# Down projection of a hybrid encoder block: more pairs of k-tiles by seven block products, and one low part per pair made by an adding transfer

## The chip, the cores and the metric

The kernel runs on one core of one Trainium2 chip. The metric is device time in microseconds of one execution. The profile of an execution gives its span (from the first to the last instruction), which is a little shorter than the time of the same execution.

## The reference

One layer of an encoder block on 256 tokens of width 2048, all in float32: a mixer (input projection, a state-space scan in two directions, a pooling mixer, output projection), a gated feed-forward with a short convolution, and a gated per-layer embedding. Each part ends in an RMS norm and is added to the residual. The change touches the down projection of the feed-forward, a product of (256 x 5632) and (5632 x 2048):

```python
def conv_glu(hn, w_up, conv_w, conv_b, w_down):
    up = hn @ w_up
    gate, val = jnp.split(up, 2, axis=-1)
    gate = dwconv_centred(gate, conv_w, conv_b)
    return (jax.nn.gelu(gate, approximate=True) * val) @ w_down
```

## The kernel before

**Products in two parts.** TensorE multiplies float32r, a shorter format. Every operand x is split into a high part (x rounded) and a low part (x minus the high part), and a product is the sum of three: high by high, high by low, low by high. `split` (L138) does this for weights: ScalarE writes the high part (L147), VectorE subtracts (L148). High and low parts go to two rings of five buffers each (tags whi and wlo), 1024 columns wide.

**Down projection.** `sublayer` (L701) is called for it at L827. It makes the 2048 output columns in two halves of 1024 (`dn0` and `dn1` in the profile's names). In each half `token_major` (L240) goes through the 44 tiles of 128 rows of the weight in 22 pairs. One pair is one load of 1 MB by SyncE (`raw`, L151, three buffers; the transfer is issued at L118). 128 tokens are one block of an activation tile, so a pair of k-tiles is a 2 x 2 by 2 x 2 block product: two token halves, two k-tiles, two column halves of 512.

**Eight or seven products.** An ordinary pair takes eight block products. With three matmuls each that is 24 matmuls of 128 x 128 by 128 x 512, in the order of the k-tiles (L256 to L262). The pairs named in `fast` go to `seven_products` (L201), a Strassen-like scheme with 21 matmuls: the first split (a, L206) and the second (b, L207) take parts of the weight as they are, then VectorE forms three differences in place in the raw buffer (L209 to L211), and two more splits (c and d) take the results. The partial sums go to the accumulators `acc` and to four more (`alt`), which `combine` (L222) adds up. The combination stands behind the pair after the last fast one; that pair, and the last of the half, run output tile by output tile (first case of the order at L256), so both k-tiles are wanted early.

**Activations.** `get_hid` (L779) makes high and low parts of the hidden activations for one pair: ScalarE copies (L783), VectorE subtracts (L784), in a tile `hs` with two buffers. Seven-product pairs also need sums of token blocks: `hid_sums` (L800) makes them with four small VectorE steps (L812 to L815, tile `hd`) and splits them (L817, L818). Those of the first four fast pairs are kept for the second half of the columns (tile `hsum`), others are made anew (tile `he`).

**Order.** Each engine runs its instructions in an order fixed when the program is built, by a scheduler with estimated costs; an instruction that waits holds up all behind it on its engine. GpSimd issues no transfer; during the down projection it does next to nothing.

Of the kernel before, what the change touches and what calls it, by code (L numbers as in the profile page):

```python
# [12 lines left out]
F32R = mybir.dt.float32r  # L13
AF = mybir.ActivationFunctionType
ALU = mybir.AluOpType

P = 128
# [6 lines left out]
NF = DFF // P  # L24
# [27 lines left out]
def build(nc, a, out):  # L52
# [5 lines left out]
    with tile.TileContext(nc) as tc, \  # L58
# [8 lines left out]
        def ins(r):  # L67
            return getattr(r, "ins", r)

        def page(name, dtype=F32):  # L70
            return gp.tile([P, 2048], dtype, tag="pg", bufs=13, name=name)
# [4 lines left out]
        def tiny(name, n=2):  # L76
            return sp.tile([P, n], F32, tag="tiny", bufs=40, name=name)

        def main(name):
            return [pm.tile([P, 512], F32, tag="main", name=f"{name}_{i}") for i in range(2)]  # L80

        def misc(name):
            return pc.tile([P, 512], F32, tag="misc", name=name)

        def mm(o, lhsT, rhs, start, stop):
            nc.tensor.matmul(o, lhsT, rhs, start=start, stop=stop, skip_group_check=True)  # L86
# [17 lines left out]
        acc, acc2 = [main(f"dtu{t}") for t in range(2)], main("dtu2")  # L104
# [10 lines left out]
        def load(dst, src, ahead=False):  # L115

            with tc.issue_after(last["dma"]) if last and not ahead else nullcontext():
                return ins(nc.sync.dma_start(dst, src))  # L118
# [17 lines left out]
        spare = {}  # L136

        def split(name, src, nel, cuts=()):  # L138

            if name in spare:  # L140
                hi, lo = spare.pop(name)
            else:
                hi = wp.tile([P, 1056], F32R, tag="whi", bufs=5, name=f"{name}h")
                lo = wp.tile([P, 1056], F32R, tag="wlo", bufs=5, name=f"{name}l")
            for c0, c1 in zip((0, *cuts), (*cuts, nel)):
                s = slice(c0, c1)
                last["act"] = ins(nc.scalar.copy(hi[:, s], src[:, s]))  # L147
                last["dve"] = ins(nc.vector.tensor_sub(lo[:, s], src[:, s], hi[:, s].bitcast(F32)))  # L148
            return hi, lo

        def raw(name, src, a_, b_):  # L151
            r = wp.tile([P, 2048], F32, tag="raw", bufs=3, name=name)
            last["dma"] = load(r[:, :a_ * b_].rearrange("p (a b) -> p a b", a=a_), src, True)
            return r
# [34 lines left out]
        def aside():  # L189

            for job in (work.pop(0) if work else ()):
                job()

        def columns(acc):

            c = 0
            for o in acc:
                yield o, c
                c += o.shape[-1]

        def seven_products(name, r, a_, acc, alt, start, stop):  # L201

            v = r.rearrange("p (b c) -> p b c", b=4)
            b11 = split(f"{name}a", r[:, :512], 512)  # L206
            b2 = split(f"{name}b", r[:, 1024:], 1024)  # L207

            nc.vector.tensor_sub(v[:, 0:2], v[:, 1::2], v[:, 0:2])  # L209
            nc.vector.tensor_sub(v[:, 3], v[:, 3], v[:, 0])  # L210
            nc.vector.tensor_sub(v[:, 2], v[:, 2], v[:, 3])  # L211
            t13 = split(f"{name}c", r[:, :1024], 1024)
            t42 = split(f"{name}d", r[:, 1024:], 1024)
            for x, (wh, wl), c, o, own in (
                    ("a11", b11, 0, alt[0], True), ("a12", b2, 0, acc[0][0], False), ("s4", b2, 512, acc[0][1], False),
                    ("s1", t13, 0, alt[1], True), ("s3", t13, 512, alt[2], True), ("a22", t42, 0, acc[1][0], False),
                    ("s2", t42, 512, alt[3], True)):
                xh, xl = a_[x]
                for q, (xx, ww) in enumerate(((xh, wh), (xh, wl), (xl, wh))):
                    mm(o, xx, ww[:, c:c + 512], own and start and q == 0, own and stop and q == 2)  # L220
# [16 lines left out]
            add(s165, alt[2], s165)  # L237
            add(acc[1][1], acc[1][1], s165)

        def token_major(name, w, c0, ks, get, acc, tail=1, fast=(), alt=None, sums=None):  # L240


            group, nu = [], len(ks) // 2
            for u in range(nu):
                k0 = ks[2 * u]
                r = raw(f"{name}r{k0}", w[k0 * P:(k0 + 2) * P, c0:c0 + 1024]
                        .rearrange("(k p) c -> p k c", p=P), 2, 1024)
                if u in fast:
                    seven_products(f"{name}{k0}", r, sums(k0), acc, alt, u == fast[0], u == fast[-1])
                    continue  # L250
                for j in range(2):
                    group.append((k0 + j, *split(f"{name}{k0}_{j}", r[:, j * 1024:(j + 1) * 1024], 1024)))
                if nu - tail <= u < nu - 1:
                    continue

                order = [(t, o, g, q) for t in range(2) for o in columns(acc[t]) for g in group for q in range(3)] \  # L256
                    if u == nu - 1 or u - 1 in fast[-1:] else \
                    [(t, o, g, q) for g in group for t in range(2) for q in range(3) for o in columns(acc[t])]
                for t, (o, c), (k, wh, wl), q in order:
                    xh, xl = (v[:, t * P:(t + 1) * P] for v in get(k))  # L260
                    xx, ww = ((xh, wh), (xh, wl), (xl, wh))[q]
                    mm(o, xx, ww[:, c:c + o.shape[-1]], k == ks[0] and q == 0, k == ks[-1] and q == 2)  # L262
                if u - 1 in fast[-1:]:
                    combine(name, acc, alt)
                group = []
                aside()
# [121 lines left out]
        for u in range(0, NK, 2):  # L388
            r = [wp.tile([P, 2048], F32, tag="raw", bufs=3, name=f"dtur{u}") if u else r0, page(f"dtur{u + 1}")]
            for j in range(2):  # L390
                k = u + j
# [17 lines left out]
            for j in range(2):  # L409
                k = u + j  # L410
                with tc.issue_after(front[0]), tc.issue_after(front[1]):
                    wh, wl = split(f"dtu{k}", r[j][:, :1056], 1056, ((352, 704), (704,))[k] if k < 2 else ())
                if k == 8:
                    half = last["act"], last["dve"]
# [250 lines left out]
        for t in range(2):  # L665
# [13 lines left out]
            r = rms(f"yn{t}", [ss], rz[t][:, 1:2], n=2)  # L679
# [18 lines left out]
            load(g, src.partition_broadcast(P))  # L698
            return g

        def sublayer(name, w, ks, get, gain, h, vnext, panel=Panel, fast=((), ()), sums=None):  # L701

            mg = [page(f"{name}m{t}") for t in range(2)]
            sq = [[], []]
            for half in range(2):

                alt = main(f"{name}s{half}") if fast[half] and half == 0 else []
                acc = [main(f"{name}a{half}{t}") for t in range(2)]
                if fast[half]:
                    alt += (main(f"{name}s{half}") if half else []) + [misc(f"{name}s{half}_{i}") for i in (2, 3)]  # L710
                token_major(f"{name}{half}", w, half * 1024, ks, get, acc, 1, fast[half], alt, sums)
                for t in range(2):
                    for n in range(2):
                        q = tiny(f"{name}q{t}{half}{n}", 1)
                        junk = sp.tile([P, 512], F32, tag="junk", bufs=1, name=f"{name}j{t}{half}{n}")
                        c = slice(half * 1024 + n * 512, half * 1024 + (n + 1) * 512)
                        b = acc[t][n]
                        nc.scalar.activation(junk, b, AF.Square, accum_out=q)
                        nc.vector.tensor_mul(mg[t][:, c], b, gain[:, c])
                        sq[t].append(q)  # L720
            r = [rms(f"{name}{t}", sq[t], 1.0 / D) for t in range(2)]
            pan = panel(f"{name}x")
            for c in range(4):
                s = slice(c * 512, (c + 1) * 512)
                for t in range(2):
                    nc.vector.scalar_tensor_tensor(h[t][:, s], mg[t][:, s], r[t], h[t][:, s],  # L726
                                                   op0=ALU.mult, op1=ALU.add)
                panel_part(f"{name}x", pan, h, vnext, 4 * c, 4 * c + 4)
            return pan
# [15 lines left out]
        h = [page(f"h{t}") for t in range(2)]  # L745
# [10 lines left out]
        for s in range(DFF // 512):  # L756
            sc = mid(f"gr{s}")
            for i in range(2):
                ga = main(f"ga{s}{i}")
                feature_pairs(f"ug{s}{i}", w_up, s * 512 + i * 256, hf, ga)  # L760
                o = sc[:, i * 512:(i + 1) * 512]
# [7 lines left out]
            for i in range(2):  # L769
                va = main(f"va{s}{i}")  # L770
                feature_pairs(f"uv{s}{i}", w_up, DFF + s * 512 + i * 256, hf, va)
                c0 = (s % 2) * 1024 + i * 512
# [27 lines left out]
        def hid_sums(k):  # L800
# [20 lines left out]
            else:  # L821
# [3 lines left out]
            return d  # L825

        hp = sublayer("dn", w_down, list(range(NF)), hid_get, gload("gffn", a["ffn_norm_post"][0]), h, V_PN,  # L827
                      fast=((2, 5, 8, 11, 14, 17), (2, 5, 8, 11, 14, 17, 19)), sums=hid_sums)


        pl.append(ple(1))
# [32 lines left out]
        for half in range(2):  # L864
            acc = [main(f"gt{half}{t}") for t in range(2)]
# [9 lines left out]
            for t in range(2):  # L875
                for n, (o, c0) in enumerate(columns(acc[t])):
                    c1 = c0 + o.shape[-1]
                    c = slice(half * 1024 + c0, half * 1024 + c1)
# [63 lines left out]
```

## Time and profile before

| | |
|---|---|
| median of 3 runs | 1146.65 us (1146.38 to 1147.1) |
| the profiled execution's own time | 1147.28 us |
| its span | 1145.5 us |
| mean granted TensorE clock | 0.994 |
| the down projection's matmuls on the chain of waits | from 801.24 to 1034.06 us |
| HBM read | 215.95 MB |

Times are microseconds from the start of the span. PE is TensorE, PEld its weight loads, DVE is VectorE, ACT ScalarE, POOL GpSimd, SP SyncE; `L86` is a line of the kernel, and as one helper records all matmuls, they are told apart by their tiles (`dna` the accumulators `acc`, `dns` those of `alt`). "x48" is a count. In a row of the chain of waits the first two numbers are start and duration; in a row of a time line a bracket names idle time before the instruction and what ended it. In a row of the groups of one tile, three durations in ns are the least, the median and the greatest.

### The profile page before, as it was taken

How to read it: one execution, taken by the hardware profiler on the slowest of the kernel's cores; microseconds unless marked ns; L12 is line 12 of the kernel's file. 1: busy time of each engine (PE TensorE's matmuls, PEld its weight loads, DVE VectorE, ACT ScalarE, POOL GpSimd, SP SyncE). 2: the span in 40 equal slices, each digit the busy share in tenths (PEclk: the TensorE clock that was granted, in tenths of full speed). 3: DMA queues.
4: the chain of work that ended last, by engine and by line, in shares of the span. 5: the costliest groups of instructions: out<-in, count | busy, mean ns of one | idle time of the engine just before them, and what ended most of it. 6: DMA issues, size and time to landing. Idle time of an engine off the chain costs nothing.

```text
span 1145.5 us, 15408 instructions
## 1 busy us (share of the span) xinstructions
PE 1126.3 (98%) x6057; PEld 971.6 (85%) x6057; DVE 824.8 (72%) x1060; ACT 598.3 (52%) x812; POOL 122.5 (11%) x123
## 2 busy tenths in 40 slices
PE   9998999999999999999999999999999999999996
PEld 9997987888888888888888888888888888887885
DVE  6578896654777665666766766668888888898573
ACT  7533543553675454544544545545555556657462
POOL 0274504200110000000000000000000000002001
PEclk9998999999999999999999999999999999999998
DMA  9952347546365555555555565556466646564752
GB/s 358 337 184 74 111 150 267 201 156 216 121 213 186 192 192 195 190 185 184 184 187 193 181 207 189 184 184 221 159 209 221 204 163 221 187 206 159 226 179 74
DMA packets 129592, 219.03 MB, mean 191 GB/s; under 512 B 3696, under 2 KB 96752, under 8 KB 128624
## 3 DMA queue, kind: packets, MB, share of 16 engines
q1 hardware_dynamic: 129232, 217.70, 57.4%
q8 instruction: 47, 0.77, 0.3%
q10 hardware_dynamic: 288, 0.36, 0.1%
q14 instruction: 25, 0.20, 0.1%
HBM read 215.95 MB, written 2.10 MB: 190 GB/s over the span
## 4 chain that ended last, share of the span: by engine, by line
PE 92%; DVE 5%; POOL 1%; ACT 1%; issue 1%; POOLq 0%; DVEq 0%; ACTq 0%
PE va L86 21%; PE ga L86 21%; PE dna L86 17%; PE woa L86 8%; PE gt L86 7%; PE dtu L86 4%; PE z L86 4%; PE xbc L86 3%; PE dns L86 3%; DVE cv L373 2%; DVE w L586 1%; DVE xb_0l L148 1%; PE ple L86 1%; PE yd L86 0%; DVE h L726 0%
## 5 line engine op out<-in xcount | busy, mean ns | idle before, releaser
L86 PE MATMUL ga<-wox,ug_0h 128*128 128x512 f32 x352 | 125.5, 395 | 0.0
L86 PE MATMUL ga<-wox,ug_1h 128*128 128x512 f32 x352 | 125.1, 394 | 0.0
L86 PE MATMUL va<-wox,uv_0h 128*128 128x512 f32 x352 | 124.8, 393 | 0.0
L86 PE MATMUL va<-wox,uv_1h 128*128 128x512 f32 x352 | 124.8, 393 | 0.0
L86 PE MATMUL ga<-wox,ug_0l 128*128 128x256 f32 x352 | 99.1, 282 | 0.0
L86 PE MATMUL ga<-wox,ug_1l 128*128 128x256 f32 x352 | 99.1, 282 | 0.0
L86 PE MATMUL va<-wox,uv_0l 128*128 128x256 f32 x352 | 99.1, 281 | 0.0
L86 PE MATMUL va<-wox,uv_1l 128*128 128x256 f32 x352 | 99.1, 281 | 0.0
L86 PEld LDWEIGHTS va<-wox,uv_0h 128*128 128x128 f32 x352 | 66.1, 188 | 15.0
L86 PEld LDWEIGHTS va<-wox,uv_1h 128*128 128x128 f32 x352 | 66.1, 188 | 15.0
L86 PEld LDWEIGHTS ga<-wox,ug_1h 128*128 128x128 f32 x352 | 66.1, 188 | 14.9
L86 PEld LDWEIGHTS ga<-wox,ug_0h 128*128 128x128 f32 x352 | 66.1, 188 | 14.8
L86 PE MATMUL dna<-dn_0h,hs 128*128 128x512 f32 x248 | 75.8, 393 | 0.0
L86 PE MATMUL dna<-dn_1h,hs 128*128 128x512 f32 x248 | 75.6, 393 | 0.0
L767 POOL TENSOR_TENSOR fc<-fc,rfb 128x1024 f32<-128x1024 f32 x11 | 26.4, 2404 | 440.2 <-ACT fc L766 440.2
L86 PEld LDWEIGHTS ga<-wox,ug_0l 128*128 128x128 f32 x352 | 66.2, 188 | 0.1
L86 PEld LDWEIGHTS ga<-wox,ug_1l 128*128 128x128 f32 x352 | 66.2, 188 | 0.0
L86 PEld LDWEIGHTS va<-wox,uv_0l 128*128 128x128 f32 x352 | 66.2, 188 | 0.0
L86 PEld LDWEIGHTS va<-wox,uv_1l 128*128 128x128 f32 x352 | 66.2, 188 | 0.0
L86 PEld LDWEIGHTS dna<-dn_1h,hs 128*128 128x128 f32 x248 | 46.5, 188 | 10.8
L86 PEld LDWEIGHTS dna<-dn_0h,hs 128*128 128x128 f32 x248 | 46.5, 188 | 10.7
L86 PE MATMUL dna<-dn_0l,hs 128*128 128x512 f32 x124 | 40.2, 393 | 0.0
(1075 smaller groups left out, 2860.3 us busy)
## 6 DMA issues: line engine op xcount, KB each, us to landing
dn0r<-w_ffn_down SPq DMA_DIRECT2D x22, 1024.0 KB, 5.5
dn1r<-w_ffn_down SPq DMA_DIRECT2D x22, 1024.0 KB, 5.5
zr<-w_in SPq DMA_DIRECT2D x8, 1024.0 KB, 5.2
wo0r<-w_out SPq DMA_DIRECT2D x8, 1024.0 KB, 5.6
wo1r<-w_out SPq DMA_DIRECT2D x8, 1024.0 KB, 5.5
gt0r<-w_ple_gate SPq DMA_DIRECT2D x8, 1024.0 KB, 6.0
gt1r<-w_ple_gate SPq DMA_DIRECT2D x8, 1024.0 KB, 5.6
dtur<-w_in SPq DMA_DIRECT2D x14, 528.0 KB, 8.6
```

The source lines that it names most:

```text
L86: nc.tensor.matmul(o, lhsT, rhs, start=start, stop=stop, skip_group_check=True)
L148: last["dve"] = ins(nc.vector.tensor_sub(lo[:, s], src[:, s], hi[:, s].bitcast(F32)))
L373: nc.vector.scalar_tensor_tensor(o[:, lo:hi], i[:, lo + d:hi + d], vec(wcol + j * wstep + f), o[:, lo:hi], op0=ALU.mult, op1=ALU.add)
L586: nc.vector.scalar_tensor_tensor(w[:, h * P:(h + 1) * P], cbm[:, 0, g, t, :], dt[:, t, 8 * g + h:8 * g + h + 1], w[:, h * P:(h + 1) * P], ...
L767: nc.gpsimd.tensor_tensor(cv.rearrange("p (f t) -> p f t", f=4), cv.rearrange("p (f t) -> p f t", f=4), rfb.unsqueeze(1).to_broadcast([P, ...
```

## The change

Three things change, all in the down projection.

- The lists `fast` name 9 and 10 pairs for 6 and 7: every second pair from 2 to 18 in both halves, and 19 in the second.
- The new list `far` names pairs 2 to 21 of the first half and all of the second. In these, one split of 1024 columns per pair, the second k-tile's (in a seven-product pair the split b), is made by the new function `split_far`: ScalarE writes the negated rounded weight into the low buffer, GpSimd issues a transfer of 512 KB that reads the same weights from HBM again and adds them to it, and ScalarE writes the high part. VectorE has no step in this split.
- `token_major` and `sublayer` hand the list on.

```diff
+        def split_far(name, src, far, nel):
...
+                hi = wp.tile([P, 1056], F32R, tag="whi", bufs=5, name=f"{name}h")
+                lo = wp.tile([P, 1056], F32R, tag="wlo", bufs=5, name=f"{name}l")
+            nc.scalar.activation(lo[:, :nel], src[:, :nel], AF.Copy, scale=-1.0)
+            o = lo[:, :nel]
+            if len(far.shape) == 3:
+                o = o.rearrange("p (k c) -> p k c", k=far.shape[1])
+            nc.gpsimd.dma_start(o, far, accum_op=ALU.add)
+            nc.scalar.copy(hi[:, :nel], src[:, :nel])
+            return hi, lo
...
-            b2 = split(f"{name}b", r[:, 1024:], 1024)
+            b2 = split(f"{name}b", r[:, 1024:], 1024) if far is None else split_far(f"{name}b", r[:, 1024:], far, 1024)
...
                 if u in fast:
-                    seven_products(f"{name}{k0}", r, sums(k0), acc, alt, u == fast[0], u == fast[-1])
+                    seven_products(f"{name}{k0}", r, sums(k0), acc, alt, u == fast[0], u == fast[-1],
+                                   w[(k0 + 1) * P:(k0 + 2) * P, c0:c0 + 1024] if u in far else None)
                     continue
                 for j in range(2):
-                    group.append((k0 + j, *split(f"{name}{k0}_{j}", r[:, j * 1024:(j + 1) * 1024], 1024)))
+                    k, s = k0 + j, r[:, j * 1024:(j + 1) * 1024]
+                    group.append((k, *(split_far(f"{name}{k0}_{j}", s, w[k * P:(k + 1) * P, c0:c0 + 1024], 1024)
+                                       if j and u in far else split(f"{name}{k0}_{j}", s, 1024))))
...
-                      fast=((2, 5, 8, 11, 14, 17), (2, 5, 8, 11, 14, 17, 19)), sums=hid_sums)
+                      fast=((2, 4, 6, 8, 10, 12, 14, 16, 18), (2, 4, 6, 8, 10, 12, 14, 16, 18, 19)), sums=hid_sums,
+                      far=(range(2, NF // 2), range(NF // 2)))
```

More of the change, by code (lines that the diff above doesn't have):

```diff
@@ L149, in split @@
             return hi, lo
+        def split_far(name, src, far, nel):
+            if name in spare:
+                hi, lo = spare.pop(name)
+            else:
+                hi = wp.tile([P, 1056], F32R, tag="whi", bufs=5, name=f"{name}h")
[7 more added lines that the diff above has]
+            return hi, lo
         def raw(name, src, a_, b_):
@@ L199, in columns, with seven_products @@
                 c += o.shape[-1]
-        def seven_products(name, r, a_, acc, alt, start, stop):
+        def seven_products(name, r, a_, acc, alt, start, stop, far):
             v = r.rearrange("p (b c) -> p b c", b=4)
             b11 = split(f"{name}a", r[:, :512], 512)
-            b2 = split(f"{name}b", r[:, 1024:], 1024)
+            b2 = split(f"{name}b", r[:, 1024:], 1024) if far is None else split_far(f"{name}b", r[:, 1024:], far, 1024)
             nc.vector.tensor_sub(v[:, 0:2], v[:, 1::2], v[:, 0:2])
@@ L238, in combine, with token_major @@
             add(acc[1][1], acc[1][1], s165)
-        def token_major(name, w, c0, ks, get, acc, tail=1, fast=(), alt=None, sums=None):
+        def token_major(name, w, c0, ks, get, acc, tail=1, fast=(), alt=None, sums=None,
+                        far=()):
             group, nu = [], len(ks) // 2
@@ L699, in gload, with sublayer @@
             return g
-        def sublayer(name, w, ks, get, gain, h, vnext, panel=Panel, fast=((), ()), sums=None):
+        def sublayer(name, w, ks, get, gain, h, vnext, panel=Panel, fast=((), ()), sums=None, far=((), ())):
             mg = [page(f"{name}m{t}") for t in range(2)]
@@ L710, in sublayer @@
                     alt += (main(f"{name}s{half}") if half else []) + [misc(f"{name}s{half}_{i}") for i in (2, 3)]
-                token_major(f"{name}{half}", w, half * 1024, ks, get, acc, 1, fast[half], alt, sums)
+                token_major(f"{name}{half}", w, half * 1024, ks, get, acc, 1, fast[half], alt, sums, far[half])
                 for t in range(2):
```

## The prediction

> **What bounds the kernel now.** I read the page first, then the chain of waits in order of time, then the table of stretches, and only then the two engines that prepare the weights.
>
> ```profile
> span 1145.5 us, 15408 instructions
> PE 1126.3 (98%) x6057; PEld 971.6 (85%) x6057; DVE 824.8 (72%) x1060; ACT 598.3 (52%) x812; POOL 122.5 (11%) x123
> GB/s 358 337 184 74 111 150 267 201 156 216 121 213 186 192 192 195 190 185 184 184 187 193 181 207 189 184 184 221 159 209 221 204 163 221 187 206 159 226 179 74
> PE va L86 21%; PE ga L86 21%; PE dna L86 17%; PE woa L86 8%; PE gt L86 7%; PE dtu L86 4%; PE z L86 4%; PE xbc L86 3%; PE dns L86 3%; DVE cv L373 2%; DVE w L586 1%; DVE xb_0l L148 1%; PE ple L86 1%; PE yd L86 0%; DVE h L726 0%
> ```
>
> TensorE is busy for 98% of the span, and the chain that ended last runs through matmuls. The down projection is "PE dna" and "PE dns" in it, a fifth of the span. Here are one ordinary stretch (two eight-product pairs) and one seven-product pair, then the table of stretches for the same 16 us and for the whole stage:
>
> ```profile
> 849.06 11.11 PE dna L86 x48
> 860.17 0.70 PE dns L86 x3
> 860.86 1.38 PE dna L86 x6
> 862.24 1.39 PE dns L86 x6
> 863.62 0.69 PE dna L86 x3
> 864.31 0.69 PE dns L86 x3
> ```
>
> ```profile
> 849.06:865.00 15.94, 15.94 (x70) 12.95 (x70) 13.21 (x15) 9.28 (x12) 0.00 (x0) 1.00 0.60 197
> 790.00:1035.00 245.00, 245.00 (x1078) 199.81 (x1077) 214.45 (x263) 145.37 (x186) 1.29 (x4) 1.00 0.59 193
> ```
>
> In the second fence the columns are PE, PEld, DVE, ACT and POOL busy, then the granted clock, DMA share and GB/s. TensorE has no gap at a clock of 1.00, so one matmul is worth 11.11 / 48 = 0.231 us. An eight-product pair (24 matmuls) takes 5.55 us, a seven-product pair (21) 4.85 us. VectorE is at 13.21 of 15.94: it is the engine with least room. The stage ends with TensorE, so only matmuls or new gaps between them change the time.
>
> **The change, part by part.** *Matmuls.* Six more pairs (13 to 19) lose three matmuls each: 18 x 0.231 = **4.2 us less**. That is all there is to win; everything else can only hold or spoil it. The two combinations stay.
>
> *VectorE.* Its rows inside one seven-product pair, where starts lie closer than durations:
>
> ```profile
> 850.55 0.68 DVE L784 TENSOR_TENSOR hs<-hid,hs 128x512 fp32r<-128x512 f32 x1
> 851.16 0.68 DVE L148 TENSOR_TENSOR dn022al<-dn0r,dn022ah 128x512 fp32r<-128x512 f32 x1
> 851.88 1.23 DVE L209 TENSOR_TENSOR dn0r<-dn0r 128x1024 f32<-128x1024 f32 x1
> 853.02 1.22 DVE L148 TENSOR_TENSOR dn022bl<-dn0r,dn022bh 128x1024 fp32r<-128x1024 f32 x1
> 854.27 0.69 DVE L210 TENSOR_TENSOR dn0r<-dn0r 128x512 f32<-128x512 f32 x1
> 855.00 0.69 DVE L211 TENSOR_TENSOR dn0r<-dn0r 128x512 f32<-128x512 f32 x1
> ```
>
> A 1024-wide step takes 1.14 us of the engine (851.88 to 853.02), a 512-wide one 0.61 (850.55 to 851.16). The new repeat is one eight-product and one seven-product pair, 45 matmuls, 10.40 us. VectorE does in it 1.14 + 0.61 for the first and 0.61 x 4 + 0.12 (a small gap) + 1.14 x 3 for the second: 7.7 us; with the two low parts that the transfer now makes it would be 10.0. Pairs whose token sums are not kept add some 1.5 us: those steps are 284 and 686 ns long:
>
> ```profile
> L812 DVE TENSOR_TENSOR hd<-hid x9: 281/284/291, 771.0 to 919.1; 128x128 f32<-128x128 f32 x9
> L818 DVE TENSOR_TENSOR he<-hd,he x5: 682/686/693, 808.8 to 1001.4; 128x512 fp32r<-128x512 f32 x5
> L817 ACT CAST he<-hd x5: 605/620/622, 807.0 to 999.6; 128x512 fp32r<-128x512 f32 x5
> ```
>
> That gives 9.2 of 10.40, and would be 11.5 without the transfer. So VectorE stays hidden, and the transfer is what makes room for the six pairs.
>
> *ScalarE.* It gains a negated copy per pair, 42 in all. Its rows:
>
> ```profile
> 854.65 0.62 ACT L783 CAST hs<-hid 128x512 fp32r<-128x512 f32 x1 [1.72 <-PE dna L86]
> 855.17 1.05 ACT L147 CAST dn022ch<-dn0r 128x1024 fp32r<-128x1024 f32 x1
> 860.25 1.05 ACT L147 CAST dn_0h<-dn0r 128x1024 fp32r<-128x1024 f32 x1 [1.72 <-PE dna L86]
> 861.20 1.04 ACT L147 CAST dn_1h<-dn0r 128x1024 fp32r<-128x1024 f32 x1
> 862.15 0.61 ACT L783 CAST hs<-hid 128x512 fp32r<-128x512 f32 x1
> ```
>
> By starts, 0.96 us for 1024 and 0.52 for 512. Per 10.40 us: seven wide and three narrow copies, 8.3 us (8.8 with sums). It fits if it rarely waits.
>
> *The new wait.* The low part used to be ready one VectorE step after the high part. Now it is ready after a copy and a transfer of time T (from the copy's end to the landing, GpSimd's issue included). Buffers are few, so this closes a loop. In the changed program's order, ScalarE in a seven-product pair makes the activations' copy (hs, two buffers) ahead of the negated copy. The row at 854.65 shows what hs waits for: TensorE's end of the pair two before, 849.06 + 5.55 = 854.61. Behind it on ScalarE stand the negated copy and c and d. In the new order the pair two before is the previous seven-product pair. From its end to the end of the next one: hs 0.52, negated copy 1.05, T, then the 17 matmuls from the first that reads the low part (the fifth) to the last, 3.93, and some 0.15 for three hand-overs (0.04 at 854.65). So **the repeat is never shorter than T + 5.65**, and TensorE sees nothing while T is below 10.40 - 5.65 = **4.75 us**. The eight-product pairs form a second loop through the five high buffers: 0.95 + 0.96 + 1.05 + T + 10 matmuls 2.31 + 0.2 = T + 5.47, nearly the same. They run in parallel, so the larger counts, not the sum.
>
> *T.* No transfer here adds, and none is issued by GpSimd. The nearest rows:
>
> ```profile
> dn0r<-w_ffn_down SPq DMA_DIRECT2D x22, 1024.0 KB, 5.5
> dn1r<-w_ffn_down SPq DMA_DIRECT2D x22, 1024.0 KB, 5.5
> out<-vg SPq DMA_DIRECT2D x8, 256.0 KB, 2.7
> gffn<-ffn_norm_post SPq DMA_DIRECT2D x1, 1024.0 KB, 8.9
> ```
>
> A plain 512 KB lies between 256 KB and 1 MB: 2.7 + 2.8 / 3 = 3.6 us, the lower end. An adding one also reads its 512 KB destination, so its engines read 1 MB: 5.5 us, the nearest row. GpSimd's issue, and the weight load that starts in the same moment (SyncE's load waits for the last read of the same raw buffer, which is now the negated copy), come on top. The upper end is 8.9, the slowest 1 MB of this stretch. I take the middle, **6.25 us**, a little over the nearest row.
>
> The Trainium skill, DMA: Bandwidth & Descriptors, section "Anatomy of one DMA — SWDGE (gpsimd) path", gives a GpSimd DMA 2.0 us plus bytes / 436e3; an estimate from it for 512 KB is 3.2 us, and by it no repeat would stall. Collectives: The Full Stack, section "The bandwidth ceiling", says that an adding transfer reads two sources on the same ring and so runs at half rate; the estimate becomes 4.4 us, still just under the loop's limit. Against that, the same fit gives 4.4 us for 1 MB where this trace's row has 5.5; no run so far shows the adding itself.
>
> *The sum.* At T = 6.25 each of the 18 seven-product pairs in the alternation (nine per half) pays 6.25 - 4.75 = 1.5 us: 27 us. The pair after the alternation (19 in the first half, 20 in the second) is worked through tile by tile, so its second low part is wanted at the fifth matmul instead of the fifteenth, 2.3 us earlier, with the copies of the second loop ahead of it: 4.85 + 0.92 - 3.1 leaves T = 2.7 without a wait. Two such pairs pay 3.5 each: 7 us. The first pairs of the halves and the last pair I set at nothing, because buffers are free or two plain pairs lie between; uncovered, each costs another 1.5. Together 27 + 7 - 4.2 = **+30 us**. The profiled execution took 1147.28 us (span 1145.5); the median shown is 1146.65. So 1177.3 against the first, **1177** against the median.
>
> **The rivals.** *1. The transfer is hidden (the other side).* Where T stays under 4.75 no alternating pair waits; the two pairs at the ends pay T - 2.7 each. At the lower end, 3.6, that is 1.8 - 4.2 = -2.4 us, 1144.2; at 4.75 it is 4.1 - 4.2, no change, 1146.5; if the ends are covered too, the whole 4.2, 1142.5. It decides at T = 4.75. For it: DMA engines are busy only 0.59 of the stage. Against it: the plain 1 MB row is over the limit already. The page's fit of 3.2 to 4.4 us leads here. 22%: 14% faster, 8% no change.
>
> *2. Bytes instead of latency.* A repeat then moves two loads of 1 MB and two adding transfers that read 1 MB each, 4.2 MB; at 358 GB/s, the most that any slice of the page shows, 11.7 us. That is 1.3 us over 10.40 in some 20 repeats: +26 - 4.2, 1168; no gap would have one latency to blame, and the loads would land late as well. 12%.
>
> *3. ScalarE becomes the bound.* It has 8.8 us of work, and the two waits of 1.72 us shown above come on top if they stay: 12.2 a repeat, 1.8 x 20 - 4.2, 1179. Against it: these waits are slack in front of free buffers today. 5%.
>
> *4. A slow T that is still paid in part by slack*, between 4.75 and 5.2: 1147 to 1157. 6%, a third of it no change.
>
> **How the numbers follow.** The forecast has 55%: T from 5.2 to 8.9, 1157 to 1230 (18 x 4.15 + 2 x 6.2 - 4.2 = +83). The range runs from the whole gain, 1143, to T of about 8.6, 1225; a slower transfer and the last half microsecond of the gain are left out, some 10%. Measurement here tells 0.2%, 2.3 us, from no change. Faster 14%; no change 8 + 2 = 10%; slower 76%.
>
> **What would show it.** In the changed profile: the GpSimd transfers' time to landing (42 of 512 KB) over 4.75 us confirms the price, under it rival 1. TensorE waits before a matmul that reads a low part, released by a DMA, about 1.5 us each, in the seven-product pairs; ends of 48 or 24 matmuls moving apart from 5.55 us. VectorE must fall from 13.21 per 15.94 us to about 0.75 to 0.9 of the time or less, or its part is wrong. Rival 2 shows as a DMA share near 0.9 and loads above 8 us; rival 3 as ScalarE without idle time. I am wrong if T is short, if the loop through hs is not closed (the negated copy ahead of hs), or if GpSimd's transfers hold each other up in their queue, which would lie above my range.

## The result, and the profile after

| | before | after |
|---|---|---|
| median, us | 1146.66 (1146.38 to 1147.1, 4 runs) | 1277.21 (1276.0 to 1278.98, 4 runs) |
| ratio to before, 95% interval | | 1.1139 (1.112 to 1.1159) |
| span of the profiled execution, us | 1145.5 | 1274.2 |
| mean granted TensorE clock | 0.994 | 0.955 |
| down projection on the chain, us | 801.24 to 1034.06 (232.8) | 800.72 to 1165.16 (364.4) |

The changed kernel is 11.4% slower. The sign was forecast; the size was not: 1277 lies far above the forecast 1177 and above the range, which ended at 1225. All of the loss is in the down projection, which takes 131.6 us longer.

From the page of the changed kernel: busy time, granted clock, the queue of GpSimd's transfers, and the DMA issues with their median time to landing; then TensorE's waits in the down projection (us in total, times, longest):

```profile
PE 1162.7 (91%) x6039; PEld 992.6 (78%) x6039; DVE 813.1 (64%) x1078; ACT 648.2 (51%) x872; POOL 159.1 (12%) x165
PEclk9998999999999999999999999999887878889998
q0 software_dynamic: 6048, 22.02, 8.9%
dn0r<-w_ffn_down SPq DMA_DIRECT2D x22, 1024.0 KB, 7.1
dn_1l<-w_ffn_down POOLq DMA_DIRECT2D x23, 512.0 KB, 9.4
```

```profile
PE dna L86 <- DMA dn_1l<-w_ffn_down: 90.2, 19, 6.3
PE dna L86 <- DMA dn138bl<-w_ffn_down: 2.0, 1, 2.0
```

TensorE runs 18 matmuls fewer (6039), yet shows 36 us more of busy time, because its clock falls: the digits 8 and 7 near the end of the clock's row lie in the down projection. It waits 90.2 us for the low part `dn_1l` (the one that the eight-product pairs now get by transfer) and only once in a seven-product pair (`dn138bl`), where the prediction had expected the waits. The adding transfer takes 9.4 us to land. The loads of 1 MB, at 5.5 us before, take 7.1. On the chain of waits, which consisted of matmuls, one pattern repeats:

```profile
815.13 4.31 DMA dn_1l<-w_ffn_down
...
950.32 8.77 DMA dn_1l<-w_ffn_down
```

The chain goes from transfer to transfer. Between them it reads "issue" for some 12 us each (rows left out here), so it gives the length of a repeat but not what closes it; the time line below shows that. In the first half eight repeats lie between 815.13 and 950.32, 16.90 us each, where 45 matmuls are 10.40 us of work. One repeat in the time line, all engines (start, duration, engine, line, operation; the bracket names idle time before it and what ended it):

```profile
881.87 0.37 SPq L118 DMA_DIRECT2D dn0r<-w_ffn_down  x1
882.14 0.87 POOL L162 DMA_DIRECT2D dn_1l<-w_ffn_down  x1 [12.49 <-ACT dn_1l L158]
885.60 0.87 POOL L162 DMA_DIRECT2D dn024bl<-w_ffn_down  x1 [2.59 <-ACT dn024bl L158]
891.54 0.72 PE L86 MATMUL dna<-dn_1l,hs 128*128 128x512 f32 x2 [4.64 <-DMA dn_1l<-w_ffn_down]
892.10 1.86 PE L86 MATMUL dna<-dn_1h,hs 128*128 128x512 f32 x4
899.01 0.87 POOL L162 DMA_DIRECT2D dn_1l<-w_ffn_down  x1 [12.54 <-ACT dn_1l L158]
```

A load of 1 MB goes out at 881.87, the adding transfer 0.27 us behind it, a second adding transfer 3.5 us later. The first lands at 891.54, 9.40 us after its issue, and TensorE has stood still for 4.64 us. Then four matmuls take 1.86 us, twice their usual 0.93. The stretches of this repeat and the one before show both (PE, PEld, DVE, ACT and POOL busy, then clock, DMA share, GB/s):

```profile
865.32:882.14 16.82, 12.23 (x47) 9.48 (x46) 8.01 (x9) 8.39 (x11) 1.74 (x2) 0.90 0.73 188
878.70:882.10 3.40, 3.40 (x16) 2.76 (x15) 1.23 (x1) 3.21 (x4) 0.00 (x0) 1.00 0.03 11
886.00:891.00 5.00, 0.91 (x4) 0.38 (x3) 4.31 (x8) 1.80 (x3) 0.47 (x1) 1.00 1.02 220
892.00:893.00 1.00, 1.00 (x5) 0.77 (x4) 0.00 (x0) 0.00 (x0) 0.00 (x0) 0.57 1.05 242
893.00:894.00 1.00, 1.00 (x4) 0.81 (x3) 0.00 (x0) 0.00 (x0) 0.00 (x0) 0.50 1.02 385
894.00:895.00 1.00, 1.00 (x3) 0.76 (x3) 0.00 (x0) 0.00 (x0) 0.00 (x0) 0.50 1.01 418
895.00:896.00 1.00, 1.00 (x5) 0.77 (x4) 0.00 (x0) 0.25 (x1) 0.00 (x0) 0.72 0.49 201
```

The DMA engines are full (1.02) while TensorE waits and nearly empty (0.03) just before the next transfer is issued: transfers bunch. After the gap the granted clock is 0.57, 0.50, 0.50 and 0.72 for four microseconds, which loses 0.43 + 0.50 + 0.50 + 0.28 = 1.7 us. So a repeat costs 16.87 - 10.40 = 6.5 us: 4.64 of waiting, 1.7 of slow matmuls, and a little for the hand-over.

The whole stage, in the same columns (the prediction shows this row for the kernel before, 790.00 to 1035.00):

```profile
790.00:1168.00 378.00, 285.83 (x1075) 224.42 (x1074) 206.44 (x286) 197.65 (x251) 41.53 (x52) 0.86 0.72 186
```

TensorE stands still for 378.00 - 285.83 = 92.2 us, in 20 gaps of 2.0 to 6.4 us. In the 364.4 us of the down projection it is therefore busy for 272.2 us, with matmuls that take 232.8 - 4.2 = 228.6 us at full clock. So 43.6 us go to the slower clock.

### The profile page after: what moved, and what is told of

It is laid out like the page before. It is cut to its first block, busy times and chain, and to the rows that moved or that the text cites. A ratio compares the mean times of both kernels' runs of the same rounds, so it can differ in the third digit from the quotient of the medians.

```text
span 1274.2 us, 15613 instructions
## 1 busy us (share of the span) xinstructions
PE 1162.7 (91%) x6039; PEld 992.6 (78%) x6039; DVE 813.1 (64%) x1078; ACT 648.2 (51%) x872; POOL 159.1 (12%) x165
## 3 DMA queue, kind: packets, MB, share of 16 engines
q1 hardware_dynamic: 129232, 217.70, 52.2%
## 4 chain that ended last, share of the span: by engine, by line
PE 68%; issue 17%; DMA 9%; DVE 4%; ACT 1%; POOL 1%; POOLq 0%; DVEq 0%; ACTq 0%
PE va L86 19%; PE ga L86 19%; DMA dn_1l<-w_ffn_down 8%; PE woa L86 7%; PE gt L86 6%; PE dna L86 4%; PE z L86 3%; PE dtu L86 3%; PE xbc L86 3%; DVE cv L392 2%; PE ple L86 1%; DMA dtur<-w_in 1%; DVE w L605 1%; DVE xb_0l L148 0%; PE yd L86 0%
## 5 line engine op out<-in xcount | busy, mean ns | idle before, releaser
L86 PE MATMUL dna<-dn_1l,hs 128*128 128x512 f32 x100 | 48.8, 567 | 90.2 <-DMA dn_1l<-w_ffn_down 90.2
L86 PEld LDWEIGHTS dna<-dn_1l,hs 128*128 128x128 f32 x100 | 25.3, 270 | 103.2 <-DMA dn_1l<-w_ffn_down 98.4
L86 PE MATMUL dna<-dn_1h,hs 128*128 128x512 f32 x200 | 81.7, 505 | 0.0
L86 PE MATMUL dna<-dn_0h,hs 128*128 128x512 f32 x200 | 63.4, 401 | 0.0
L86 PEld LDWEIGHTS dna<-dn_1h,hs 128*128 128x128 f32 x200 | 51.5, 258 | 13.5
```

## The experiments

My theory after the result: the closed loop of the prediction governs, its T is long because of what runs beside the transfer, and the rest is the clock. At first I took the second adding transfer of a repeat for what lengthens T; the loads took its place after the kernel with transfers in eight-product pairs alone. The rivals: the denser sequence of seven-product pairs costs the time; the adding itself does; the bytes alone are too many. Line numbers below are those of the kernel in question.

**Two halves of the change, apart.** First the longer lists without the transfer (dense):

```diff
-                      fast=((2, 4, 6, 8, 10, 12, 14, 16, 18), (2, 4, 6, 8, 10, 12, 14, 16, 18, 19)), sums=hid_sums,
-                      far=(range(2, NF // 2), range(NF // 2)))
+                      fast=((2, 4, 6, 8, 10, 12, 14, 16, 18), (2, 4, 6, 8, 10, 12, 14, 16, 18, 19)), sums=hid_sums)
```

> Half of the change alone: the 19 pairs by seven products, no adding transfer (all low parts by VectorE). If the transfer is the whole loss, this stays near the kernel before: the matmuls give 4.2 us, and VectorE, with 11.5 us of work per 10.40 us where token sums are made anew (11 of 19 pairs) and 10.0 elsewhere, gives some 12 us back: 1150 to 1158 us. If the denser sequence itself upsets the buffers (the rival), it is far above 1165.

Measured: 1151.34 us (5 runs, 1150.91 to 1152.21), ratio to before 1.0042 (1.0028 to 1.0056). A stretch of it:

```profile
855.00:899.00 44.00, 44.00 (x192) 35.46 (x191) 43.90 (x57) 28.69 (x38) 0.00 (x0) 1.00 0.59 192
```

VectorE has no idle time left (43.90 of 44.00), but TensorE has no gap in this stretch either (44.00). Its gaps, 4.5 us in all, stand elsewhere: 2.2 us at the two combinations, where it waits for VectorE, and 2.3 us in pair 19 of the second half. So the six pairs alone win nothing, and the sequence itself costs only 4.4 us.

Second, the transfer with the old lists of 6 and 7 pairs (far only):

```diff
-                      fast=((2, 4, 6, 8, 10, 12, 14, 16, 18), (2, 4, 6, 8, 10, 12, 14, 16, 18, 19)), sums=hid_sums,
+                      fast=((2, 5, 8, 11, 14, 17), (2, 5, 8, 11, 14, 17, 19)), sums=hid_sums,
                       far=(range(2, NF // 2), range(NF // 2)))
```

> The other half alone: the adding transfers in the same 42 pairs, but the 13 seven-product pairs of the kernel before. The theory that a wait for the transfer closes a loop gives a loss of the same kind: per repeat of three pairs (15.94 us) a time of T + 11.4 plus slow matmuls after the gap 1.6, so with T of 8 to 9.4 a repeat of 21 to 22.4, 13.5 times: 1215 to 1235 us. If the loss needed the denser sequence (DMA engines full because pairs are shorter), this is within 20 us of the kernel before.

Measured: 1253.82 us in a single run, more than expected. Its DMA issues:

```profile
dn_1l<-w_ffn_down POOLq DMA_DIRECT2D x29, 512.0 KB, 10.1
```

With no pair more by seven products the transfers alone account for 107 us, and they land as late (10.1 us) as in the whole change. The denser sequence is out as the main cause. The whole change, in which TensorE waits 20 times for a transfer and not 14 times as here, is 23 us slower still.

**Adding or moving?** The transfer copies instead of adding (plain). The subtraction of the rounded weight is left out, so the low part holds the whole weight.

```diff
-            nc.gpsimd.dma_start(o, far, accum_op=ALU.add)
+            nc.gpsimd.dma_start(o, far.bitcast(F32R))
```

> The changed kernel with a plain GpSimd transfer of the same 512 KB in place of the adding one; it leaves out the subtraction, so the low parts hold the whole weights. Orders on the engines are the same. If the adding doubles what the DMA engines do, T falls from 9.4 to about 6.5 to 7 and a repeat from 16.9 to about 14: 1200 to 1225 us. If GpSimd's way of transferring is slow whatever it does, 1277 stays.

Measured: 1231.11 us in a single run, a little above the expected. Its page, and for the prices in it the same row of the kernel before:

```profile
q0 software_dynamic: 6048, 22.02, 5.0%
dn_1l<-w_ffn_down POOLq DMA_DIRECT2D x23, 512.0 KB, 7.6
dn04bl<-w_ffn_down POOLq DMA_DIRECT2D x1, 512.0 KB, 4.3
```

```profile
q1 hardware_dynamic: 129232, 217.70, 57.4%
```

The third number of a queue's row is its packets' share of the 16 engines' span. Copying, the 42 transfers keep all engines busy for 5.0% of 1229.3 us, 1.46 us each; adding (8.9% of 1274.2) 2.70 us each, 1.85 times as much (the other kernels with adding transfers give 2.7 to 3.2 us). A load of 1 MB (1.049 of 217.70 MB, 57.4% of 1145.5 us) is 3.2 us. The rule of the Trainium skill that the prediction cited, Collectives: The Full Stack, section "The bandwidth ceiling", half rate for an adding transfer (there in a collective), is borne out nearly in full. It was not the answer, though: a plain copy still takes 7.6 us to land in the eight-product pairs, and 84 us of the loss stay.

Two successive repeats of this kernel also show how fickle the clock is: the gaps before the same matmul, and the clock behind each.

```profile
868.66 0.73 PE L86 MATMUL dna<-dn_1l,hs 128*128 128x512 f32 x2 [2.80 <-DMA dn_1l<-w_ffn_down]
882.19 1.22 PE L86 MATMUL dna<-dn_1l,hs 128*128 128x512 f32 x2 [2.82 <-DMA dn_1l<-w_ffn_down]
```

```profile
869.00:870.00 1.00, 1.00 (x6) 0.81 (x5) 0.00 (x0) 0.00 (x0) 0.00 (x0) 1.00 0.69 98
882.00:887.00 5.00, 4.81 (x11) 3.80 (x12) 0.79 (x4) 0.10 (x1) 0.00 (x0) 0.50 0.72 224
```

After 2.80 us it is 1.00, after 2.82 us 0.50 for 5 us, and the two repeats take 13.5 and 15.9 us. Of the 19 gaps of 2.47 to 4.91 us in this kernel's down projection, nine, the longest of them 3.53 us, leave the clock at 1.00 for the next 6 us; behind the other ten it is lower.

**Fewer transfers: only in seven-product pairs, or only in eight-product pairs.**

```diff
-                      far=(range(2, NF // 2), range(NF // 2)))
+                      far=(range(2, 19, 2), (*range(2, 19, 2), 19)))
```

> The changed kernel with the adding transfer in the seven-product pairs only (split b); in eight-product pairs VectorE subtracts again. This takes the second loop away and halves the added bytes. If the wait loops decide, the loop through hs remains: a repeat of T + 5.65 with T about 6.5 with half the crowd, plus up to 1.6 for slow matmuls: 12.2 to 13.8 us, so 1175 to 1205 us. If it is bytes (DMA engines full), the added half fits into 10.40 us and the time falls to 1143 to 1150 us.

Measured: 1164.04 us (4 runs, 1162.81 to 1165.23), ratio 1.0149 (1.0134 to 1.0165), between the two expectations. Its chain and a stretch:

```profile
865.83 5.82 DMA dn024bl<-w_ffn_down
877.35 5.39 DMA dn028bl<-w_ffn_down
888.44 5.51 DMA dn032bl<-w_ffn_down
899.67 5.51 DMA dn036bl<-w_ffn_down
```

```profile
855.00:899.67 44.67, 41.94 (x179) 32.91 (x178) 39.50 (x51) 31.56 (x39) 2.83 (x5) 1.00 0.90 232
```

From start to start the repeats are 11.52, 11.09 and 11.23 us; less the landing times (5.82, 5.39, 5.51) that leaves 5.70, 5.70 and 5.72, where the prediction had T + 5.65. The length fits, but the loop is not the one through `hs`. What ScalarE waits for after the landing at 871.65, and the last load ahead of the transfer:

```profile
861.93 0.37 SPq L118 DMA_DIRECT2D dn0r<-w_ffn_down  x1
874.52 1.05 ACT L163 CAST dn028bh<-dn0r 128x1024 fp32r<-128x1024 f32 x1 [0.71 <-PE dns L86]
875.48 0.61 ACT L802 CAST hs<-hid 128x512 fp32r<-128x512 f32 x1
```

The copy into the high buffer `dn028bh` waits for TensorE, until 11 matmuls after the landing have freed its buffer of the ring of five. The copy of `hs` stands behind it and has no wait of its own. From the landing on that is 0.04 + 2.81 + 0.02 + 0.96 (to the start of `hs`) + 0.51 + 1.06 (the negated copy) + 0.30 (to the issue) = 5.70 us. That this loop is as long as the one forecast through `hs` is luck. T, counted from the issue, is 5.4 to 5.8 us in these repeats (6.7 and 6.9 us in two others), near the row of 5.5 us of the kernel before. The last load stands 3.9 us ahead of the transfer (861.93), and not 0.27 us as in the changed kernel. In this stretch the gaps are 0.4 to 0.9 us, and the clock stays at 1.00; behind the two longest of the stage, 1.82 and 1.98 us, it is 0.72 over the next 6 us. Now the other choice:

```diff
-                      far=(range(2, NF // 2), range(NF // 2)))
+                      far=((*range(3, 19, 2), 19, 20, 21), (0, *range(1, 19, 2), 20, 21)))
```

> The mirror of the run with the transfer in seven-product pairs only: dense lists, adding transfer in eight-product pairs only. The loop through the high buffers stays: repeat T + 5.5. By the theory that T alone is 5.5 and 9.4 only because two adding transfers and the loads crowd each other, T is 5.7 to 6.7 here (a load starts in the same moment), a repeat 11.2 to 12.2: 1160 to 1185 us. If this place is simply the bad one whatever else runs (T stays 9.4), 1250 or more.

Measured: 1300.26 us in a single run, worse than the whole change, and a clear miss. Its time line:

```profile
870.56 0.37 SPq L118 DMA_DIRECT2D dn0r<-w_ffn_down  x1
872.15 0.37 SPq L118 DMA_DIRECT2D dn0r<-w_ffn_down  x1
872.42 0.86 POOL L162 DMA_DIRECT2D dn_1l<-w_ffn_down  x1 [17.93 <-PE dna L86]
882.24 1.22 PE L86 MATMUL dna<-dn_1l,hs 128*128 128x512 f32 x2 [5.25 <-DMA dn_1l<-w_ffn_down]
886.01 0.62 ACT L802 CAST hs<-hid 128x512 fp32r<-128x512 f32 x1 [9.25 <-PE dna L86]
890.74 0.86 POOL L162 DMA_DIRECT2D dn_1l<-w_ffn_down  x1 [17.45 <-PE dns L86]
```

There is one adding transfer per 18.3 us, with none near it, and it still takes 9.8 us. That fells the theory on which the expectation rested, that two adding transfers hold each other up. What does stand ahead of it are two loads of 1 MB, 1.9 and 0.3 us earlier. This kernel also got another order on ScalarE: the copy of `hs` at 886.01 waits 9.25 us for TensorE, with the next pair's copies queued behind it, so its loop, which here does run through `hs`, is longer as well. How the extra time divides between the two was not separated.

**Is it the loads?** The weights of the first three pairs of each half are loaded and used again for all later pairs (no loads). Left out are the other loads, so that most products use an earlier pair's weights; the adding transfers stay, 3.5 us apart as before.

```diff
-                r = raw(f"{name}r{k0}", w[k0 * P:(k0 + 2) * P, c0:c0 + 1024]
-                        .rearrange("(k p) c -> p k c", p=P), 2, 1024)
+                if fast and len(old) == 3:
+                    r = old[u % 3]
+                else:
+                    r = raw(f"{name}r{k0}", w[k0 * P:(k0 + 2) * P, c0:c0 + 1024]
+                            .rearrange("(k p) c -> p k c", p=P), 2, 1024)
+                    old.append(r)
```

> The changed kernel without most loads of the down projection: after the first three pairs of each half the raw buffers keep what they have, so 6 loads of 1 MB are left of 44 and the sums are not the reference's. The order on the engines is the same. If T is 9.4 because loads released in the same moment share the DMA engines, T falls to 5.5 to 6.5 and a repeat to 11.2 to 12.5: 1160 to 1190 us. If the two adding transfers of a repeat, 3.5 us apart, hold up each other, T stays near 9 and the time above 1250.

Measured: 1187.56 us in a single run, at the upper end of the expected. Time to landing, and the time line:

```profile
dn_1l<-w_ffn_down POOLq DMA_DIRECT2D x23, 512.0 KB, 5.6
```

```profile
861.65 0.88 POOL L162 DMA_DIRECT2D dn_1l<-w_ffn_down  x1 [7.15 <-ACT dn_1l L158]
865.10 0.88 POOL L162 DMA_DIRECT2D dn024bl<-w_ffn_down  x1 [2.58 <-ACT dn024bl L158]
867.06 0.73 PE L86 MATMUL dna<-dn_1l,hs 128*128 128x512 f32 x2 [0.47 <-DMA dn_1l<-w_ffn_down]
872.99 0.88 POOL L162 DMA_DIRECT2D dn_1l<-w_ffn_down  x1 [7.01 <-ACT dn_1l L158]
```

```profile
908.26 8.70 DMA dn_1l<-w_ffn_down
```

Without loads T falls from 9.4 to 5.6 us and the gap from 4.64 to 0.47 us, with the same 42 transfers in the same queue. So the loads make T long. The last row, from the chain, shows it inside this kernel: at 908.26, where a load of the next half stands 0.27 us ahead again, the transfer takes 8.7 us. That the loads do it by filling the 16 DMA engines is argued from the share of 1.02 in the changed kernel. The repeat (861.65 to 872.99) is 11.34 us; the second loop of the prediction gives 5.41 + 0.30 from the copy's end to the issue + 5.47 = 11.2. The kernel is still 41 us slower than the one before: its 15 repeats lose some 17 us, and the ends of the halves, where other loads do run, most of the rest (gaps of 5.38, 4.75, 2.10, 1.68 and 4.82 us and the clock behind them).

**Is it the clock?** In the changed kernel, 20 matmuls with a block of zeros in place of the activations go in ahead of the wait in 18 eight-product pairs; pairs 19 to 21 are left as they are (fill).

```diff
+        zero = cp.tile([P, P], F32R, name="zero")
+        nc.scalar.activation(zero, ident, AF.Copy, scale=0.0)
...
+                    if far and u in far and group[0][0] != k and (t, c, q) == (0, 0, 1) and u not in (19, 20, 21):
+                        for _ in range(20):
+                            mm(o, zero, wh[:, :512], False, False)
```

> The changed kernel with 20 matmuls by a tile of zeros (4.6 us, they add nothing) put into the gap ahead of the first low-part product of the alternating eight-product pairs, 18 gaps. If the matmuls after the gap are slow because TensorE had stood idle (granted clock 0.57 in that stretch), they run at 0.23 us again and a repeat falls from 16.9 to about 15.2: 18 x 1.6 = 29 us less, 1245 to 1252. If they are slow because full DMA engines hold up TensorE's reads, nothing is won: 1277 or more.

Measured: 1254.80 us in a single run: with 360 matmuls more, the kernel is 22 us faster. Stretch and landing time:

```profile
825.00:890.00 65.00, 65.00 (x282) 52.41 (x281) 34.64 (x42) 36.93 (x44) 6.96 (x8) 1.00 0.81 213
```

```profile
dn_1l<-w_ffn_down POOLq DMA_DIRECT2D x23, 512.0 KB, 9.1
```

TensorE has no gap and the clock is 1.00, while the transfer is about as slow as before (9.1 us). So the slow matmuls come from the idle time, not from the transfers that run beside them. The repeat is 15.1 us, just its 65 matmuls, so the 22 us are a lower bound of what the clock costs in the changed kernel, for which its own trace gave 43.6 us.

**Taking the transfer off the loop.** As in the kernel with transfers in seven-product pairs alone, and the matmuls that read the low part of split b stand at the end of their pair (low last), so that the transfer has 15 matmuls, some 3.5 us, more:

```diff
+            late = []
...
+                    if far is not None and ww is b2[1]:
+                        late.append((o, xx, ww[:, c:c + 512]))
+                        continue
...
+            for o, xx, ww in late:
+                mm(o, xx, ww, False, False)
...
-                      far=(range(2, NF // 2), range(NF // 2)))
+                      far=(range(2, 19, 2), (*range(2, 19, 2), 19)))
```

> The kernel with the adding transfer in seven-product pairs only, and their two products with that low part moved to the end of the pair. This opens the loop: behind the first use of the low part stand 2 matmuls instead of 17, so the loop is T + 2.2 or less, 7.7 us with T of 5.5, and the wait should vanish. VectorE has 8.9 us per repeat (10.4 with new sums). If the wait is all that the version with the transfer in seven-product pairs loses, 1143 to 1148; if VectorE holds up the pairs with new sums as in the run without any transfer, 1148 to 1152; if the bytes matter, above 1155.

Measured: 1143.38 us (6 runs, 1142.93 to 1145.56) against 1147.13 (10 runs) of the kernel before, ratio 0.9973 (0.9961 to 0.9985). It is 0.3% faster than that kernel and 1.8% faster than the one without this order. Its stretch and one of its transfers:

```profile
849.00:870.00 21.00, 21.00 (x93) 17.05 (x92) 19.53 (x27) 16.23 (x20) 1.92 (x3) 1.00 0.94 258
```

```profile
dn024bl<-w_ffn_down POOLq DMA_DIRECT2D x1, 512.0 KB, 8.3
```

TensorE is dense although the transfer takes 8.3 us: a long transfer is harmless off the loop. The 3.75 us won are nearly the 4.2 us of matmuls. The same order for the matmuls without any transfer is the check on that (order only):

```diff
-                    if far is not None and ww is b2[1]:
+                    if ww is b2[1]:
...
-                      far=(range(2, 19, 2), (*range(2, 19, 2), 19)))
```

> Control for the version that moved the low products to the end of the seven-product pairs: the same order and the same 19 pairs, but no transfer, VectorE makes every low part. If that version wins because the transfer takes work off VectorE and is no longer waited for, this one stays at VectorE's bound, 1149 to 1153 us. If the order alone is what wins, 1143 to 1145.

Measured: 1151.32 us (5 runs), ratio 1.0038 (1.0025 to 1.0052), the same as the dense kernel. Order alone wins nothing; it needs the transfer that relieves VectorE.

**All 42 transfers, with their matmuls last** (all late): the same edit as low last, all of `far`, and in the eight-product pairs:

```diff
+                if far and u in far and not (u == nu - 1 or u - 1 in fast[-1:]):
+                    order = [i for i in order if i[3] != 1 or i[2] is group[0]] + \
+                        [i for i in order if i[3] == 1 and i[2] is not group[0]]
```

> The changed kernel, all 42 transfers, with the products by those low parts moved to the end of each pair (four matmuls in an eight-product pair, two in a seven-product pair). If only the loops cost, they shrink to about T + 4.0: with T still 9.4 a repeat of 13.4 without gaps long enough to slow TensorE: 1195 to 1215. If the DMA engines are the floor under it (two loads of 3.2 us and two adding transfers of 2.7 us of all engines, 11.8 us a repeat), it cannot fall under 1170.

Measured: 1184.54 us in a single run, between the two expectations. Stretch and one gap:

```profile
860.00:900.00 40.00, 37.39 (x155) 29.73 (x154) 29.09 (x41) 31.10 (x38) 6.10 (x7) 0.96 1.01 265
873.00:874.00 1.00, 1.00 (x4) 0.71 (x4) 0.15 (x1) 0.21 (x1) 0.00 (x0) 0.50 1.03 274
```

```profile
872.09 1.67 PE L86 MATMUL dna<-dn_1l,hs 128*128 128x512 f32 x4 [2.12 <-DMA dn_1l<-w_ffn_down]
```

The DMA share is 1.01 over the whole 40 us. Per repeat the engines have two loads and two adding transfers to do, 2 x 3.2 + 2 x 2.7 = 11.8 us; the repeat is 11.9 us (three of them from 862.51 to 898.27). By this estimate there is a floor under the loop: with 42 transfers no order of the matmuls gets to 10.40 us.

## Why the prediction was wrong

- **Matmuls**, -4.2 us: right. 18 fewer matmuls run, and where nothing else stands in the way (low last) 3.75 us are won.
- **VectorE and ScalarE**: right. Per repeat they were to have 7.7 to 9.2 and 8.3 to 8.8 us; the stretch shows 8.01 and 8.39, and the next one, with new sums, 9.32 and 8.92. VectorE did need the relief: without the transfer it is full (43.90 of 44.00 us, dense), and in the same order of matmuls the transfer wins 7.9 us (low last against order only).
- **The loop**: a closed loop sets the repeat, as forecast, but the one that was put first, through `hs`, is not the one. In the changed kernel 19 of TensorE's 20 waits for a transfer stand in the eight-product pairs, and ScalarE waits for TensorE with the high buffer `dn_0h`. This is the forecast's second loop, at its length: 9.40 + 0.30 + 5.47 is 15.2, and the ten matmuls inside it take 3.9 us for 2.3, which makes 16.8; the trace has 16.82 to 16.87. The kernel with no loads shows it without the slow clock. The prediction set both loops nearly equally long (T + 5.65 and T + 5.47), so the mistake cost its number little.
- **T: the step that failed.** "I take the middle, 6.25 us, a little over the nearest row." By that definition, from the copy's end, T is 9.7 us. The nearest row was the right price for a transfer with no load released beside it: 5.4 to 5.8 us (far only in seven-product pairs), 5.6 us (no loads). The prediction named the load that starts in the same moment and then gave it three quarters of a microsecond. But that load brings 3.2 us of work for all engines, the adding transfers 2.7 each, and once the loop stalls TensorE, buffers come free and transfers start in bunches: share 1.02 in the gap, 0.03 just ahead. A mean DMA share of 0.59 before the change said nothing about the share in those 9 us. With T = 9.7 the prediction's own sum gives 18 x 4.95 + 2 x 7.0 = 103 us of waiting, where 92.2 were measured, and with the 4.2 us of matmuls taken off +99.
- **The clock: a term that was missing.** The prediction let every matmul behind a wait run at full clock. In the changed kernel 43.6 us of the stage are matmuls at a lower clock, and 92.2 + 43.6 - 4.2 is the measured 131.6. The Trainium skill, TensorE: Matmul & The Clock Gate, section "HAM oscillation — how this bites in real kernels", describes this case: a wait for a transfer of 3 to 5 us lets the clock fall to half, and the next group of matmuls runs throttled for some 1.67 us, of which half is lost, each time round. The traces agree on the two states (0.50 and 1.00) but not on the size: here some 4 us run at a lower clock, and 1.7 us and more are lost. They differ on the bound too: the page, in "What's actually happening", asks for an idle window of about 3.4 us, and here gaps of 1.82 us (far only in seven-product pairs), 2.12 us (all late) and 2.82 us (plain) were enough, while one of 3.53 us (plain) was not.
- **Ends**: sized too low with T. The 15 repeats on the chain at 16.9 and 17.3 us make 100 us; the rest of the stage, its first pairs, the turn between the halves and the last pairs, makes 36, where the prediction had 11.5. Of these, 22.6 us are five gaps (5.45, 6.35, 5.36, 2.01 and 3.47 us), and the remaining 13 are matmuls at a lower clock. The gap of 6.35 us stands in the last pair of the first half, which the prediction set at nothing.
- **Rivals.** The bytes (1168 by a floor of 11.7 us a repeat) are real but lie under the loop; they show as 11.9 us once the loop is opened. The hidden transfer came true in a kernel that the change is not: low last. ScalarE never became the bound. Transfers holding each other up in GpSimd's queue, which the prediction named as what would lead above its range, is ruled out as the cause on its own: with the queue unchanged and the loads gone, T is 5.6 us.

## What to carry to other kernels

Before a transfer goes onto a path where its landing gates the next issue, price it with everything that is released in the same moment, and not by its time alone or by a mean DMA share: here 5.5 us became 9.4. Count with a lower clock behind new TensorE gaps of some 2 us or more: here 20 of them cost 43.6 us on top of 92.2 us of waiting, though in the kernel with the plain copy nine of 19 cost nothing. And where a late operand is needed by few of the products, moving those to the end of their group may hide what no faster transfer would: 1143.4 us instead of 1164.0 with the same transfers.

## What was not expected of the hardware

- After a gap of 4.64 us the granted clock was 0.50 to 0.72 for about 4 us. A gap of 1.82 us could lower it, and one of 3.53 us did not have to. Filling the gaps with idle products kept it at 1.00 and made the kernel 22 us faster.
- An adding transfer of 512 KB takes 2.70 us of all 16 engines, a copying one 1.46 us. In pair 2 of the first half, where the last load is issued 3.7 us ahead and the next one only after the landing, the adding one lands after 5.5 us and the copying one after 4.3 us. The issue of an adding one holds GpSimd for 0.87 us.
- The same adding transfer lands after 5.4 us without loads (no loads, 861.65) and after 9.40 us with a load of 1 MB issued 0.27 us ahead of it, a second adding transfer 3.5 us and another load 7.6 us behind it.
